# Three pooled means from bands in four buffers with alternating halves, and the decays of linear attention two chunks at a time

## The chip, the cores and the metric

The kernel runs on one core of a Trainium2 chip. The metric is the device time of one launch in microseconds (us), and lower is better. The engines that matter here are TensorE (PE, with its weight loads shown apart as PEld), VectorE (DVE), ScalarE (ACT), GpSimd (POOL) and the DMA queue of SyncE (SP), from which nearly all transfers of this kernel are issued.

## The reference

The reference runs two transformer blocks on 512 latent tokens of width 1024, and in the first block on 256 context tokens too. The change touches the first block alone, which has two layers (0 and 1). The mixer of a layer concatenates three parts and multiplies them by `w_out`: a pooled mean, gated linear attention, and softmax attention of the latent tokens over latent and context keys.

```python
mix = jnp.concatenate([pool_mixer(p, w_pool, s_pool),
                       gla_output(o_gl, gg, g_gla, x.dtype),
                       latent_attention(ql, k_all, v_all)], axis=-1) @ w_out
x = x + ga1 * mix
```

`pool_mixer` takes 256 features in four groups of 64. Each group has a window of its own (2, 4, 8 or 16 tokens); its mean over the window minus the token itself is multiplied by a 64x64 matrix and scaled:

```python
for gi, w in enumerate(POOL_WINDOWS):
    lo = np.clip(t - w // 2, 0, N - 1)
    hi = np.clip(t + w // 2 - 1, 0, N - 1)
    cnt = jnp.asarray((hi - lo + 1)[None, :, None], jnp.float32)
    mean = (Pg[:, hi + 1] - Pg[:, lo]) / cnt
    outs.append(mean - pf[:, :, gi])
```

Gated linear attention has decays `la = log_sigmoid(r @ w_gate + b_gate) / 16`, which are summed up along a chunk; the state is multiplied by the exponential of a chunk's sum from one chunk to the next, forward and backward:

```python
b = jnp.cumsum(lc, axis=2)
S_new = jnp.exp(bl[:, :, 0, :, None]) * S + jnp.einsum('bhjd,bhje->bhde', kc * jnp.exp(bl - b), vc)
```

## The kernel before

Activations are kept transposed, with features on the partitions, and each large product is done as three matmuls of split operands (`dense`, L296 to L298 and their token-major forms; below they are called dense work). The program is written as one list of steps. A scheduler then fixes the order of the instructions on each engine; the engines run their own lists in that order, and wait for each other and for transfers by semaphores. SP's list is such a list too: a DMA whose buffer isn't free yet holds up every DMA behind it.

**The pooled mean** (`pool`, L998 to L1031) is a product with band matrices that hold window, count and the minus one. For each group of 64 features it loads one band tile `bt` of 128x400 (L1008: three variants of a 128x128 band; L1009 and L1010: two edges of eight columns), and for each block of 128 tokens it does one matmul of 128 columns (L1017) and up to two of eight columns for what reaches over the block's edge (L1021, L1024). Two groups share a PSUM bank: one takes partitions 0 to 63, the other 64 to 127. The tag `bt` has one buffer. The two banks come from the tag `mm`, which has two in all and is the one that dense work uses too. Afterwards the two banks are copied (L249, L251), multiplied by the 64x64 matrices in block form (L1030) and scaled (L1031).

`pool` is called three times: for the context in layer 0 (256 tokens, two blocks), for the latents in layer 0 (512 tokens, four blocks), and for the latents in layer 1, in program order behind that layer's attention.

**Around it in layer 0** the kernel still computes the modulation vectors in pieces (L448 loads a quarter of a piece into `mraw`, which has two buffers; L451 multiplies; L460 folds; L462 adds). They all pass through the single bank `at`, as the keys (L865) and the transposed weights (L942) of the context's attention do. The first norm of the latents (L368, L404) takes its sums in the `mm` banks, too. Behind it the dense projections of the latents start.

**Attention** (`attend`) goes through blocks of four heads: scores (L926, L927), row maximum (L928), exponential (L936), transposes through `at` and `op` (L942) into a tile `PT` of six buffers (`weights`, L933), and products with the values (L952), four `PT` tiles a block. In layer 1 it has eight blocks of four heads.

**The decays** (`gla_states`, `sums`) are made chunk by chunk of 128 tokens: Abs (L634), Exp (L635), Ln (L636), four scans (L640), the chunk's sum (L642) and its exponential `dec` (L643). ACT needs an `ACT_TABLE_LOAD` where functions of different tables follow each other.

Of the kernel before, what the change touches and what calls it, by code (L numbers as in the profile page):

```python
# [14 lines left out]
AF = mybir.ActivationFunctionType  # L15
# [177 lines left out]
class Kern:  # L193
# [423 lines left out]
    def gla_states(self, l, o, n, init):  # L617

        nc = self.nc
        nch = n // 128  # L620
        h4 = lambda a: a.rearrange("p (h t) -> p h t", h=4)
        dec = []
        space = self.t([128, 8, 256], "gst")
        bg = self.vec(f"bg{l}")
        o["tot"] = []
        def sums(c):

            zp = self.sm()
            for hh in range(4):
                nc.tensor.matmul(zp[:, hh * 128:(hh + 1) * 128], self.wg[:, hh * 128:(hh + 1) * 128],  # L630
                                 o["r"][:, c * 128:(c + 1) * 128], start=True, stop=True)
            y, a, B = self.w("K"), self.w("Q"), o["B"][c]
            nc.vector.tensor_tensor(h4(y), h4(zp), bg.unsqueeze(2).to_broadcast([128, 4, 128]), op=ALU.add)
            nc.scalar.activation(a, y, AF.Abs)  # L634
            nc.scalar.activation(a, a, AF.Exp, scale=-1.0)  # L635
            nc.scalar.activation(a, a, AF.Ln, bias=1.0)  # L636
            nc.vector.scalar_tensor_tensor(y, y, 0.0, a, op0=ALU.min, op1=ALU.subtract)
            for hh in range(4):
                nc.vector.tensor_tensor_scan(h4(B)[:, hh], self.ones, h4(y)[:, hh], 0.0, op0=ALU.mult, op1=ALU.add)
            tot = self.t([128, 4], "tot", 10)  # L640
            nc.vector.tensor_scalar(tot, h4(B)[:, :, 127], 1.0 / 16, None, op0=ALU.mult)
            d = self.t([128, 4], "dec", 10)  # L642
            nc.scalar.activation(d, tot, AF.Exp)  # L643
            nc.vector.tensor_tensor(B[64:], B[64:], y[64:], op=ALU.subtract)
            dec.append(d)
            o["tot"].append(tot)

        def update(c):

            B, tot = o["B"][c], o["tot"][c]  # L650
            EK = self.w("E")
            for hh in range(4):
                nc.scalar.activation(h4(EK)[:64, hh], h4(B)[:64, hh], AF.Exp, scale=-1.0 / 16, bias=tot[:64, hh:hh + 1])
            nc.scalar.activation(EK[64:], B[64:], AF.Exp, scale=1.0 / 16)
            nc.vector.tensor_tensor(EK, EK, o["kd"][c], op=ALU.mult)
            tp = self.sm()
            for hh in range(4):
                s = slice(hh * 128, (hh + 1) * 128)
                nc.tensor.transpose(tp[:, s], EK[:, s], self.ident)
            KT = self.w("QE")  # L660
            self.copy(KT, tp)
            up = self.sm()
            for hh in range(4):
                nc.tensor.matmul(up[:, hh * 64:(hh + 1) * 64], KT[:, hh * 128:(hh + 1) * 128],
                                 o["gv"][c][:, hh * 64:(hh + 1) * 64], start=True, stop=True)
            self.copy(space[:, 4 + c], up[:, :256])
        sums(0)
        for c in range(nch):
            if c + 1 < nch:
                sums(c + 1)  # L670
            update(c)
        d4 = lambda a: a.rearrange("p (h e) -> p h e", h=4)
        S = [space[:, c] for c in range(nch)]
        fin = self.t([128, 256], "Sfin", 2)
        for half, order in ((slice(0, 64), range(nch)), (slice(64, 128), range(nch - 1, -1, -1))):
            order = list(order)
            if init is None:
                nc.gpsimd.memset(S[order[0]][half], 0.0)
            else:
                nc.vector.tensor_copy(S[order[0]][half], init[half])  # L680
            for i, c in enumerate(order):
                dst = S[order[i + 1]] if i + 1 < nch else fin
                nc.vector.tensor_tensor(d4(dst[half]), d4(S[c][half]),
                                        dec[c][half].unsqueeze(2).to_broadcast([64, 4, 64]), op=ALU.mult)
                nc.vector.tensor_tensor(dst[half], dst[half], space[half, 4 + c], op=ALU.add)
        o["S"] = S
        return fin
# [310 lines left out]
    def pool(self, l, o, n, out):  # L998

        nc = self.nc  # L1000
        ntb = n // 128
        sums = [self.ps()[:, :n] for _ in range(2)]
        for pr in range(2):
            ps = sums[pr]
            for half in range(2):
                gi = pr * 2 + half
                bt = self.t([128, 400], "bt")
                nc.sync.dma_start(bt[:, :384], self.A["bands"][:, gi * 384:(gi + 1) * 384])  # L1008
                nc.sync.dma_start(bt[:, 384:392], self.A["bands"][:, 1536 + gi * 8:1536 + gi * 8 + 8])  # L1009
                nc.sync.dma_start(bt[:, 392:400], self.A["bands"][:, 1568 + gi * 8:1568 + gi * 8 + 8])  # L1010
                r = slice(half * 64, half * 64 + 64)
                ch = slice(gi * 64, gi * 64 + 64)
                for tb in range(ntb):
                    v = 0 if tb == 0 else 2 if tb == ntb - 1 else 1
                    t0 = tb * 128
                    more = (tb > 0) + (tb < ntb - 1)
                    nc.tensor.matmul(ps[r, t0:t0 + 128], o["p"][tb][:, ch], bt[:, v * 128:(v + 1) * 128],  # L1017
                                     start=True, stop=False, skip_group_check=True)
                    if tb > 0:
                        more -= 1  # L1020
                        nc.tensor.matmul(ps[r, t0:t0 + 8], o["p"][tb - 1][:, ch], bt[:, 384:392],  # L1021
                                         start=False, stop=(more == 0), skip_group_check=True)
                    if tb < ntb - 1:
                        nc.tensor.matmul(ps[r, t0 + 120:t0 + 128], o["p"][tb + 1][:, ch], bt[:, 392:400],  # L1024
                                         start=False, stop=True, skip_group_check=True)
        for pr in range(2):
            self.copy(out[pr], sums[pr])
        for pr in range(2):
            yp = self.ps()[:, :n]
            nc.tensor.matmul(yp, self.wp[:, pr], out[pr], start=True, stop=True)  # L1030
            nc.scalar.activation(out[pr], yp, AF.Copy, scale=self.vec(f"s_pool{l}")[:, pr:pr + 1])  # L1031
# [46 lines left out]
    def block1(self):  # L1078
        nc, A = self.nc, self.A
# [21 lines left out]
        def finish(l, j, n, x, hm, hid, tags):  # L1101
# [11 lines left out]
            elif j == 0:  # L1113
# [10 lines left out]
        o = dict(gv=self.take(U, 0, 2, 256), kd=self.take(U, 512, 2, 512), qd=self.take(U, 1536, 2, 512),  # L1124
                 B=self.take(U, 2560, 2, 512), p=self.take(U, 3584, 2, 256), aq0=self.take(U, 4608, 2, 256),
                 aq1=self.take(U, 5120, 2, 256), gg=self.take(U, 5632, 2, 256),
                 kv=self.take(U, 4096, 2, 256), kvs=[U[:, 4096:4608]],
                 aqs=[U[:, 4608:5120], U[:, 5120:5632]])
        self.gla_proj(0, h, NC, o)
        self.masks(o["gv"][1])  # L1130
        self.after(o["gv"][1], self.t([128, 400], "bt")[:, :1])
        self.att_proj(0, h, NC, o)
        self.rest_proj(0, h, NC, o)
        self.ropes(o["gg"][1])
# [35 lines left out]
        for l in range(2):  # L1170
            if l == 0:
                h, U, o = hl, Ul, ol
                self.gla_proj(0, h, NL, o)
            else:
                h, U = self.hpairs(), self.ground()
                first_norm(1, 0, NL, x, h, self.NORM, SPLITS["down0"])
                V, o = arrays(U)
# [14 lines left out]
            if l == 0:  # L1192
# [17 lines left out]
                o = dict(gv=self.take(U, 0, 2, 256), kv=self.take(U, 512, 2, 256), kd=self.take(U, 2048, 2, 512),  # L1210
                         B=self.take(U, 5120, 2, 512), kvs=[U[:, 512:1024]])
# [691 lines left out]
```

## Time and profile before

| what | value |
|---|---|
| median of 3 runs | 3540.68 us (3539.99 to 3544.39) |
| the profiled execution | 3541.75 us, of which 3539.7 us from the first to the last instruction |
| mean granted TensorE clock | 0.961 of full speed |
| busy share of PE, PEld, DVE, ACT, POOL | 94%, 79%, 60%, 46%, 2% |
| instructions | 53711 |

The busy share of PE is an average over the kernel. It is lower in a few stretches of the first block, and the three calls of `pool` lie at 121 to 140 us (context), 247 to 272 us (latents, layer 0) and 1366 to 1388 us (latents, layer 1). A matmul's duration in the rows is longer than the distance to the next one, since matmuls are pipelined; the work that PE does in a stretch is read from the distances of the starts.

### The profile page before, as it was taken

The page shows a single profiled execution, that of the slowest core. Times are in us where ns is not written, and L with a number is a line of the kernel's source. Part 1 is how long each engine was busy: PE and PEld are TensorE (multiplying, and loading weights), DVE is VectorE, ACT ScalarE, POOL GpSimd, SP SyncE. Part 2 cuts the span into 40 slices and gives each one's busy share as a digit, 9 for nine tenths or more (in the row PEclk, how much of TensorE's full clock was granted, in tenths as well). Part 3 has the DMA queues.
Part 4 walks back from the last instruction along what each step waited for, and adds up shares of the span by engine and source line. Part 5 has one row for each costly group of instructions (what it writes and reads, how often), then busy time and mean ns, then how long its engine had stood idle before and what let it go on. Part 6 is the DMA issues. An engine that isn't in the chain of part 4 may idle for free. (4 is left out here: it accounts for less than half of the span.)

```text
span 3539.7 us, 53711 instructions
## 1 busy us (share of the span) xinstructions
PE 3330.4 (94%) x20698; PEld 2811.5 (79%) x20698; DVE 2130.1 (60%) x3914; ACT 1635.7 (46%) x3023; POOL 59.4 (2%) x105
## 2 busy tenths in 40 slices
PE   7898799998999999889999899999999999999998
PEld 5776788887788788777788687778889877888886
DVE  3833898557533448856533668999766436563334
ACT  3513766354333346633333557666554325364332
POOL 0000000000000000000000000000000000000000
PEclk9799899999999999999999899999999999999998
DMA  6443122744632321036632357565666556553222
GB/s 226 136 159 100 60 85 72 238 151 132 194 115 96 109 66 44 9 108 194 201 106 89 112 159 225 169 183 158 206 194 190 176 169 202 159 180 119 95 95 72
DMA packets 267247, 491.44 MB, mean 139 GB/s; under 512 B 44784, under 2 KB 128752, under 8 KB 266736
## 3 DMA queue, kind: packets, MB, share of 16 engines
q1 hardware_dynamic: 212976, 446.06, 39.7%
q10 hardware_dynamic: 54016, 41.95, 3.6%
q8 instruction: 163, 2.67, 0.3%
q14 instruction: 92, 0.75, 0.1%
HBM read 430.11 MB, written 57.80 MB: 138 GB/s over the span
## 5 line engine op out<-in xcount | busy, mean ns | idle before, releaser
L286 DVE TENSOR_TENSOR wlo<-wraw,whi 128x1024 fp32r<-128x1024 f32 x503 | 615.2, 1223 | 574.7 <-ACT whi L285 563.2
L285 ACT ACTIVATE whi<-wraw 128x1024 fp32r<-128x1024 f32 x503 | 531.4, 1056 | 911.9 <-PE mm L297 776.9
L296 PE MATMUL mm<-h,whi 128*128 128x512 f32 (+1 forms) x2344 | 862.0, 370 | 30.8 <-ACT h L419 8.4
L297 PE MATMUL mm<-h,whi 128*128 128x512 f32 (+1 forms) x2344 | 854.0, 365 | 16.9 <-DVE h L420 13.1
L298 PE MATMUL mm<-h,wlo 128*128 128x512 f32 (+1 forms) x2344 | 838.4, 365 | 7.8 <-DVE wlo L286 7.7
L296 PEld LDWEIGHTS mm<-h,whi 128*128 128x128 f32 x2344 | 447.6, 192 | 113.6 <-ACT h L419 11.5
L297 PEld LDWEIGHTS mm<-h,whi 128*128 128x128 f32 x2344 | 449.0, 192 | 94.8 <-DVE h L420 20.9
L298 PEld LDWEIGHTS mm<-h,wlo 128*128 128x128 f32 x2344 | 446.2, 191 | 81.3 <-DVE wlo L286 10.7
L296 PE MATMUL mm<-whi,h 128*128 128x256 f32 x1200 | 350.7, 295 | 11.2 <-ACT whi L285 8.3
L297 PE MATMUL mm<-wlo,h 128*128 128x256 f32 x1200 | 349.7, 292 | 11.8 <-DVE wlo L286 11.4
L298 PE MATMUL mm<-whi,h 128*128 128x256 f32 x1200 | 345.3, 289 | 0.0
L296 PEld LDWEIGHTS mm<-whi,h 128*128 128x128 f32 x1200 | 231.0, 194 | 28.1 <-ACT whi L285 10.6
L297 PEld LDWEIGHTS mm<-wlo,h 128*128 128x128 f32 x1200 | 232.6, 194 | 21.9 <-DVE wlo L286 17.9
L298 PEld LDWEIGHTS mm<-whi,h 128*128 128x128 f32 x1200 | 232.2, 193 | 14.1 <-issue 11.2
L296 PE MATMUL mm<-U,whi 128*128 128x512 f32 (+1 forms) x608 | 229.1, 377 | 3.2 <-DVE V L1075 3.2
L297 PE MATMUL mm<-U,whi 128*128 128x512 f32 (+1 forms) x608 | 227.2, 374 | 0.0
L298 PE MATMUL mm<-U,wlo 128*128 128x512 f32 (+1 forms) x608 | 223.8, 377 | 0.0
L488 DVE SCALAR_TENSOR_TENSOR AT<-mraw,cst,AT 128x512 f32<-128x512 f32 x140 | 105.0, 750 | 100.7 <-DMA mraw<-in_w_ada 62.0
L1285 DVE SCALAR_TENSOR_TENSOR fa<-fr,const,fa 128x511 f32<-128x511 f32 (+2 forms) x192 | 142.9, 753 | 22.8 <-ACT fa L1280 20.3
L296 PE MATMUL mm<-big,whi 128*128 128x512 f32 x384 | 153.2, 399 | 2.7 <-DVE fa L1817 1.8
L297 PE MATMUL mm<-big,whi 128*128 128x512 f32 x384 | 152.8, 398 | 0.0
L298 PE MATMUL mm<-big,wlo 128*128 128x512 f32 x384 | 149.2, 397 | 0.0
(531 smaller groups left out, 5017.3 us busy)
## 6 DMA issues: line engine op xcount, KB each, us to landing
wraw<-in_w_in SPq DMA_DIRECT2D x166, 512.0 KB, 3.9
wraw<-in_w_up SPq DMA_DIRECT2D x96, 512.0 KB, 3.4
wraw<-in_w_down SPq DMA_DIRECT2D x96, 512.0 KB, 3.4
mraw<-in_w_mod SPq DMA_DIRECT2D x96, 256.0 KB, 3.1
mraw<-in_w_ada SPq DMA_DIRECT2D x96, 256.0 KB, 3.0
wraw<-in_w_out SPq DMA_DIRECT2D x40, 512.0 KB, 3.3
wraw<-in_w_mlp_up SPq DMA_DIRECT2D x40, 512.0 KB, 3.3
mraw<-in_w_late SPq DMA_DIRECT2D x64, 256.0 KB, 2.9
```

Of the source, the lines that this page charges most:

```text
L285: nc.scalar.activation(hi, raw, AF.Copy)
L286: nc.vector.tensor_tensor(lo, raw, hi.bitcast(F32), op=ALU.subtract)
L296: nc.tensor.matmul(out, lh, rh, start=start, stop=False)
L297: nc.tensor.matmul(out, lh, rl, start=False, stop=False)
L298: nc.tensor.matmul(out, ll, rh, start=False, stop=stop)
L488: nc.vector.scalar_tensor_tensor(acc, raw, st[:, k, 0:1], acc, op0=ALU.mult, op1=ALU.add)
L1285: nc.vector.scalar_tensor_tensor(acc[:, d:], raw[:, :NL - d], w(j), acc[:, d:], op0=ALU.mult, op1=ALU.add)
```

## The change

The band tiles of all four groups get buffers of their own. They are four tiles of the tag `PT`, which has six buffers and belongs to attention. Each is first written in one column by a copy on POOL from `gg[1]` (`after`, L526), so that it isn't loaded before that projection is there, and then loaded by three DMAs; all twelve DMAs are issued ahead of the matmuls. The matmuls then go over token blocks and steps, and the two groups that share a bank alternate from one instruction to the next. The number of matmuls, their sizes and their sums are what they were. A gate of the old single buffer (`after(o["gv"][1], ...)`, L1131) is gone.

In the decays, `sums` ends behind Exp, `logs` does what follows, and `pair` calls `sums` for two chunks and then `logs` for both. The exponential of the chunk's sum moves into `update`.

```diff
-        sums(0)
-        for c in range(nch):
-            if c + 1 < nch:
-                sums(c + 1)
+
+        def pair(c):
+            for i, ya in enumerate([sums(c), sums(c + 1)]):
+                logs(c + i, *ya)
+        pair(0)
+        for c in range(0, nch, 2):
+            if c + 2 < nch:
+                pair(c + 2)
             update(c)
+            update(c + 1)
...
         sums = [self.ps()[:, :n] for _ in range(2)]
+        bands = []
+        for gi in range(4):
+            bt = self.t([128, 768], "PT", 6)[:, :400]
+            self.after(o["gg"][1], bt[:, :1])
+            nc.sync.dma_start(bt[:, :384], self.A["bands"][:, gi * 384:(gi + 1) * 384])
+            nc.sync.dma_start(bt[:, 384:392], self.A["bands"][:, 1536 + gi * 8:1536 + gi * 8 + 8])
+            nc.sync.dma_start(bt[:, 392:400], self.A["bands"][:, 1568 + gi * 8:1568 + gi * 8 + 8])
+            bands.append(bt)
         for pr in range(2):
-            ps = sums[pr]
-            for half in range(2):
-                gi = pr * 2 + half
-                bt = self.t([128, 400], "bt")
...
+            for tb in range(ntb):
...
+                for i, (b, to, c) in enumerate(steps):
+                    for gi, r in both:
+                        nc.tensor.matmul(ps[r, to], o["p"][b][:, gi * 64:gi * 64 + 64], bands[gi][:, c],
+                                         start=(i == 0), stop=(i == len(steps) - 1), skip_group_check=True)
...
         self.masks(o["gv"][1])
-        self.after(o["gv"][1], self.t([128, 400], "bt")[:, :1])
```

Three places of the order show what the scheduler makes of it. The first is SP's list at the latents' pool of layer 0. A name's number is one tile: `bt_2064`, `bt_2078` are two users of the one buffer, `PT_2052` to `PT_2067` are four tiles in four buffers, `mraw` is a piece of modulation weights. In the square brackets is what the instruction waits for. Before:

```order
L1008 DMA bt_2064<-in_bands 128x384 [waits DMAHW7_49,PE_49]
L1009 DMA bt_2064<-in_bands 128x8
L1010 DMA bt_2064<-in_bands 128x8
L284 DMA wraw_3007<-in_w_in 128x1024 [waits DVE_49]
L448 DMA mraw_1172<-in_w_mod 128x512 [waits DMAHW5_49,PE_49]
L448 DMA mraw_1176<-in_w_mod 128x512 [waits DMAHW6_49,DMAHW4_49,PE_49]
L1008 DMA bt_2078<-in_bands 128x384 [waits DMAHW1_49,DMAHW7_49,DMAHW0_49,PE_49]
L1009 DMA bt_2078<-in_bands 128x8
L1010 DMA bt_2078<-in_bands 128x8
L448 DMA mraw_1180<-in_w_mod 128x512 [waits DMAHW3_49,PE_49]
```

Now:

```order
L1017 DMA PT_2057<-in_bands 128x8
L1016 DMA PT_2052<-in_bands 128x384 [waits Pool_49]
L1016 DMA PT_2057<-in_bands 128x384 [waits DMAHW3_49,Pool_49]
L1018 DMA PT_2057<-in_bands 128x8 [waits DMAHW4_49]
L1016 DMA PT_2062<-in_bands 128x384 [waits Pool_49]
L1017 DMA PT_2062<-in_bands 128x8
L1018 DMA PT_2062<-in_bands 128x8 [waits DMAHW7_49]
L1016 DMA PT_2067<-in_bands 128x384 [waits DMAHW0_49,Pool_49]
L448 DMA mraw_1112<-in_w_mod 128x512 [waits DMAHW1_49,PE_49]
L448 DMA mraw_1116<-in_w_mod 128x512 [waits DMAHW2_49,PE_49]
L1017 DMA PT_2067<-in_bands 128x8 [waits DMAHW3_49]
L1018 DMA PT_2067<-in_bands 128x8 [waits DMAHW4_49]
```

Before, each load of a band waited for PE's matmuls with the band before it, and the loads of modulation pieces stood behind it in the list. Now all four bands stand together, wait for the copies on POOL, and are in the list some 15 rows earlier.

The second place is PE's list in the same pool. `mm_2048` and `mm_2050` are the first of its two banks, `mm_2049` and `mm_2051` the second; 64x128 is a matmul of 128 columns. Before, one band's matmuls followed each other, with modulation pieces (L451, L460) between the bands, here between the second and the third:

```order
L1017 MATMUL mm_2048<-bt_2064,U_297_1469 64x128
L1021 MATMUL mm_2048<-bt_2064,U_297_1469 64x8
L460 MATMUL at_1149<-const_69,mrow_1166 128x2 x2
L451 MATMUL at_1171<-mraw_1172,cst_72 32x256 x2
L451 MATMUL at_1171<-mraw_1176,cst_72 32x256 x2
L1017 MATMUL mm_2049<-bt_2078,U_297_1469 64x128
L1024 MATMUL mm_2049<-bt_2078,U_297_1469 64x8
```

Now the two bands of a bank take turns, and the third and fourth band follow the first two at once:

```order
L1033 MATMUL mm_2050<-PT_2052,U_296_1471 64x8
L1033 MATMUL mm_2050<-PT_2057,U_296_1471 64x8
L1033 MATMUL mm_2051<-PT_2062,U_296_1471 64x128
L1033 MATMUL mm_2051<-PT_2067,U_296_1471 64x128
L1033 MATMUL mm_2051<-PT_2062,U_296_1471 64x8
L1033 MATMUL mm_2051<-PT_2067,U_296_1471 64x8
```

From the pool's first matmul to its last, ten rows of L451 and two of L460 stood between its own rows before; two of L451 and one of L460 are left there, and the others stand behind the pool now.

The third place is PE's list where layer 1's attention ends (`op_13107` and `op_13113` are the last block's products with the values, `at_...` the reciprocals of its sums, `h_...` the mixed features that go into `w_out`). Before, the pool's matmuls, both L1030 and 36 dense matmuls of 512 columns stood inside the attention, and dense work followed its end at once:

```order
L952 MATMUL op_13107<-PT_13176,V_1889_11240 64x128
L952 MATMUL op_13107<-PT_13188,V_1889_11240 64x128
L960 MATMUL at_13225<-const_69,inv_13226 128x128 x2
L296 MATMUL mm_14208<-h_2352_14169,whi_14241 128x512
L296 MATMUL mm_14209<-h_2352_14169,whi_14241 128x512
L297 MATMUL mm_14208<-h_2352_14169,whi_14241 128x512
```

Now nothing of the pool and no dense matmul of `w_out` stands inside the attention; all of the pool stands behind it, and then the dense work:

```order
L961 MATMUL op_13113<-PT_13182,V_1888_11246 64x128
L961 MATMUL op_13113<-PT_13194,V_1888_11246 64x128
L969 MATMUL at_13231<-const_69,inv_13232 128x128 x2
L1033 MATMUL mm_14075<-PT_14077,U_1865_11164 64x128
L1033 MATMUL mm_14075<-PT_14082,U_1865_11164 64x128
L1033 MATMUL mm_14075<-PT_14077,U_1865_11164 64x8
```

SP's list there, with the `PT` buffers that the last two attention blocks had (the first two tiles follow the last but one block, the other two the last):

```order
L1017 DMA PT_14077<-in_bands 128x8 [waits DVE_49,PE_49,Activation_49]
L1016 DMA PT_14077<-in_bands 128x384 [waits Pool_49]
L1018 DMA PT_14077<-in_bands 128x8 [waits DMAHW7_49]
L1016 DMA PT_14082<-in_bands 128x384 [waits DMAHW0_49,Pool_49]
L1017 DMA PT_14082<-in_bands 128x8 [waits DMAHW1_49]
L1018 DMA PT_14082<-in_bands 128x8 [waits DMAHW2_49]
L1017 DMA PT_14087<-in_bands 128x8 [waits DVE_49,DMAHW3_49,PE_49,Activation_49]
L1016 DMA PT_14087<-in_bands 128x384 [waits DMAHW4_49,Pool_49]
```

What moved here is the whole third pool, with all that has to wait for its two banks: its loads now wait for the attention's last products.

In the decays the order on ACT keeps the `ACT_TABLE_LOAD`s: 25 in the whole kernel before and 25 now. The Ln of a pair's first chunk still stands between the Exps of the two chunks, with a load on each side.

## Rows read from the trace of the kernel before

**Rows 1.** Busy time by stretch: PE, PEld, DVE, ACT, POOL; then granted clock, DMA share, GB/s.

```profile
120.00:168.00 48.00, 42.80 (x317) 33.36 (x315) 40.61 (x97) 19.23 (x50) 6.44 (x11) 0.70 0.42 135
...
247.00:280.00 33.00, 27.84 (x178) 16.79 (x179) 4.61 (x11) 3.30 (x5) 0.00 (x0) 0.64 0.49 152
...
1360.00:1530.00 170.00, 148.66 (x1386) 125.44 (x1385) 143.72 (x281) 104.99 (x242) 10.43 (x20) 0.96 0.07 20
```

**Rows 2.** Timeline of the context pool in layer 0.

```profile
121.47 0.43 PE L1017 MATMUL mm<-bt,U 128*64 128x128 f32 x2
...
129.45 0.69 PE L1017 MATMUL mm<-bt,U 128*64 128x128 f32 x2 [0.91 <-DMA bt<-in_bands]
...
139.11 0.38 ACT L249 ACTIVATE U<-mm 128x256 f32<-128x256 f32 x1 [6.01 <-PE mm L1021]
```

**Rows 3.** Timeline of PE behind it: the first dense work of the latents.

```profile
168.18 0.58 PE L296 MATMUL mm<-whi,h 128*128 128x256 f32 x1
```

**Rows 4.** SP queue's waits, 100 to 300 us: line, what for, us, times, longest.

```profile
SPq L448 <- PE at L451: 67.0, 40, 5.0
```

**Rows 5.** Timeline of the latents' pool in layer 0, all engines.

```profile
246.56 0.28 PE L297 MATMUL mm<-wlo,h 128*128 128x256 f32 x1
...
246.68 0.28 PE L298 MATMUL mm<-whi,h 128*128 128x256 f32 x1
...
246.89 0.43 PE L1017 MATMUL mm<-bt,U 128*64 128x128 f32 x2
...
247.24 0.41 PE L1017 MATMUL mm<-bt,U 128*64 128x128 f32 x2
...
247.49 0.23 PE L1021 MATMUL mm<-bt,U 128*64 128x8 f32 x2
...
247.65 0.64 PE L451 MATMUL at<-mraw,cst 128*32 128x256 f32 x8
...
252.09 1.73 PE L451 MATMUL at<-mraw,cst 128*32 128x256 f32 x8 [2.80 <-DMA mraw<-in_w_mod]
...
253.74 0.69 PE L1017 MATMUL mm<-bt,U 128*64 128x128 f32 x2
...
256.93 0.33 SPq L1008 DMA_DIRECT2D bt<-in_bands  x1
...
271.48 3.78 PE L1030 MATMUL mm<-U,lw 128*128 128x512 f32 x4
```

**Rows 6.** Landing time of the band loads (L1008).

```profile
DMA to landing us min/median/max: 2.3/2.4/3.9
```

**Rows 7.** Context attention: the scores of the 16 heads, first and last start.

```profile
L926 PE MATMUL S<-K,q x16: 279/365/582, 310.7 to 351.7; 128*128 128x256 f32 x16
```

**Rows 8.** Timeline of PE there: two heads' scores.

```profile
342.51 0.38 PE L926 MATMUL S<-K,q 128*128 128x256 f32 x1 [0.48 <-ACT P L936]
...
344.38 0.36 PE L926 MATMUL S<-K,q 128*128 128x256 f32 x1
```

**Rows 9.** Timeline of PE there: the work that follows.

```profile
360.12 1.65 PE L630 MATMUL sm<-oo,lw 128*128 128x128 f32 x6 [1.96 <-ACT oo L249]
```

**Rows 10.** Timeline of PE at the end of layer 1's attention.

```profile
1518.91 0.62 PE L296 MATMUL mm<-h,whi 128*128 128x512 f32 x2
...
1527.23 1.04 PE L952 MATMUL op<-PT,V 128*64 128x128 f32 x16
1528.10 0.61 PE L952 MATMUL op<-PT,vc 128*64 128x128 f32 x8
...
1531.68 0.73 PE L296 MATMUL mm<-h,whi 128*128 128x512 f32 x2 [1.46 <-ACT h L259]
...
1533.22 0.39 PE L297 MATMUL mm<-h,whi 128*128 128x512 f32 x1
1533.45 0.39 PE L298 MATMUL mm<-h,wlo 128*128 128x512 f32 x1
```

**Rows 11.** Table loads of Ln, by its line.

```profile
L636 ACT ACT_TABLE_LOAD  x12: 1283/1283/1283, 81.1 to 1350.3; - x12
```

More of the change, by code (lines that the diff above doesn't have):

```diff
@@ L631, in sums @@
                                  o["r"][:, c * 128:(c + 1) * 128], start=True, stop=True)
-            y, a, B = self.w("K"), self.w("Q"), o["B"][c]
+            y, a = self.w("K"), self.w("Q")
             nc.vector.tensor_tensor(h4(y), h4(zp), bg.unsqueeze(2).to_broadcast([128, 4, 128]), op=ALU.add)
@@ L635, in sums, with logs @@
             nc.scalar.activation(a, a, AF.Exp, scale=-1.0)
+            return y, a
+        def logs(c, y, a):
+            B = o["B"][c]
             nc.scalar.activation(a, a, AF.Ln, bias=1.0)
@@ L641, in sums @@
             nc.vector.tensor_scalar(tot, h4(B)[:, :, 127], 1.0 / 16, None, op0=ALU.mult)
-            d = self.t([128, 4], "dec", 10)
-            nc.scalar.activation(d, tot, AF.Exp)
             nc.vector.tensor_tensor(B[64:], B[64:], y[64:], op=ALU.subtract)
-            dec.append(d)
             o["tot"].append(tot)
@@ L650, in update @@
             B, tot = o["B"][c], o["tot"][c]
+            d = self.t([128, 4], "dec", 10)
+            nc.scalar.activation(d, tot, AF.Exp)
+            dec.append(d)
             EK = self.w("E")
@@ L1002, in pool @@
         sums = [self.ps()[:, :n] for _ in range(2)]
-        for pr in range(2):
-            ps = sums[pr]
-            for half in range(2):
-                gi = pr * 2 + half
-                bt = self.t([128, 400], "bt")
[L1008 to L1025, printed above, removed]
@@ new lines, in pool @@
+        bands = []
[6 more added lines that the diff above has]
+            bands.append(bt)
+        for pr in range(2):
+            ps, both = sums[pr], [(pr * 2 + half, slice(half * 64, half * 64 + 64)) for half in range(2)]
+            for tb in range(ntb):
+                v = 0 if tb == 0 else 2 if tb == ntb - 1 else 1
+                t0 = tb * 128
+                steps = [(tb, slice(t0, t0 + 128), slice(v * 128, (v + 1) * 128))]
+                if tb > 0:
+                    steps.append((tb - 1, slice(t0, t0 + 8), slice(384, 392)))
+                if tb < ntb - 1:
+                    steps.append((tb + 1, slice(t0 + 120, t0 + 128), slice(392, 400)))
+                for i, (b, to, c) in enumerate(steps):
+                    for gi, r in both:
+                        nc.tensor.matmul(ps[r, to], o["p"][b][:, gi * 64:gi * 64 + 64], bands[gi][:, c],
+                                         start=(i == 0), stop=(i == len(steps) - 1), skip_group_check=True)
```

## The prediction

> **What bounds the kernel now.** I read the table of busy time by stretch first, then the timeline of each stretch with a pool in it. Over the kernel PE is the bound, so only those stretches count in which PE loses time, and the table shows two of them around the first two pools [rows 1]. From 120 to 168 us PE is busy for 42.80 us, but at 0.70 of the full clock: some 30 us of work at full speed, so that 18 of 48 us are lost. From 247 to 280 us it is busy for 27.84 us at 0.64, some 18 us of work in 33 us, so that 15 us are lost. The stretch of layer 1's attention is another matter: PE 148.66, DVE 143.72 of 170 us, clock 0.96.
>
> The timelines show what the reader is to see there. The context's pool starts at 121.47 us, waits for a band at 129.45 and gives its banks free at 139.11, when the copies read them [rows 2]: 17.6 us for eight groups of matmuls. The first dense work of the latents comes at 168.18 us [rows 3], since their first norm needs the two `mm` banks that the pool holds. The latents' pool of layer 0 lasts from 246.89 to 271.48 us, where L1030 follows: 24.6 us [rows 5]. At full clock a 128-column product (two instructions) takes 0.25 us from start to start (247.24 to 247.49), and one with its eight-column product 0.35 (246.89 to 247.24), so that an edge takes 0.10. The later ones run at half clock: the row that lasted 0.43 us lasts 0.69. In between PE waits 2.80 us for a piece of modulation weights (252.09): the SP queue had not issued it yet, for it stood behind a band's loads that waited for PE. At 256.93 us the next band is issued at last, right behind the last matmul with the one before. SP's own table says the same: loads of modulation pieces waited 67.0 us for PE at L451 [rows 4]. So the pool and the modulation take turns through one queue and one buffer each, and the clock falls meanwhile.
>
> **The change, part by part.**
>
> *A, the context's pool.* The twelve loads stand early in SP's list and wait for POOL's copies only. The pool's matmuls can follow each other from 123 us or so. Eight products with eight edges are 8 x 0.35 = 2.8 us at full clock [rows 5] and 6 at half, so the banks come free near 128 instead of 139.1, 11 us earlier. The chain from there to the dense work (29 us, [rows 2, 3]) has its own waits on DVE, which is busy for 40.61 of the 48 us [rows 1], so it won't shrink much by itself. What stood in it and is now later in PE's order (some 6 us of linear attention and modulation) is hidden in dense work at first, but costs PE its time. Bounds: 0, if DVE holds the chain in place, and -18, all that is lost. I take -10, near the 11 us by which the banks are early.
>
> *B, the latents' pool, layer 0.* It has 16 products and 24 edges: 16 x 0.25 + 24 x 0.10 = 6.4 us at full clock. Eight of the ten L451 rows of the order (two rows are the x8 that took 0.64 us, [rows 5]) and an L460 of about 0.5 move behind the pool, 3.1 us of work. What is left inside, two L451 rows and an L460, is 1.1 us more, so the 24.6 us become about 6.4 + 1.1, less the alternation, and 3.1 us are paid later: -14 to -16. L1030 ran 3.78 us for four at the falling clock [rows 5]; without the fall this gives another 1 or 2. I take -16; bounds -6 (the pool still waits for its bands or for the moved pieces) and -19 (all 15 lost us and the alternation).
>
> *Alternation.* What two halves of the array do in turn is seen in L952, which has the same shape and alternates already: 16 matmuls from 1527.23 to 1528.10, 54 ns each [rows 10], against 125 ns for those of the pool at full clock (0.25 us for two, [rows 5]). For the 32 instructions of a latents' pool that is worth 32 x 0.071 = 2.3 us, and 1.1 us for the 16 of the context's. The Trainium skill, "TensorE: Matmul & The Clock Gate", Part 3: Packing small matmuls, says that a weight load overlaps matmuls in flight only when the row group differs, and these differ in the column group; by that the alternation would be worth nothing and the sum 5.7 us higher. The rows of L952 speak against it. The 2.3 and 1.1 us are within the -16 and -10 above.
>
> *What is given back in layer 0.* The pieces of modulation are later in PE's order against the dense work, and the context's attention waits for the last of them, since both use the bank `at`. So less dense work lies beside that attention: by the order 39 dense matmuls of 256 columns between L865 and the first L630 instead of 156. The 117 at 0.12 us (246.56 to 246.68, [rows 5]) are 14 us that come ahead of it now. Its 16 heads start at 310.7 and 351.7 us [rows 7], 2.7 us apart on the mean; alone they run at 1.87 us (342.51 to 344.38, [rows 8]), 31 us in all, and L630 follows at 360.12 [rows 9]. So it gets shorter by (2.73 - 1.87) x 15 = 13 us at best, which would pay for nearly all of those 14, or by nothing. I take +4, bounds 0 and +14. From there on PE is full, and what is won by L630 stays: -10 - 16 + 4 = -22.
>
> *C, the pool of layer 1.* Here `PT` decides. Two of the four tiles take buffers that the last but one attention block had, two those of the last, so the loads wait for the last products with the values. Before, dense work came back at 1531.68 us, 2 us behind the last L952, and all of the pool and 36 dense matmuls had been done inside the attention [rows 10]. Now follow, behind the end of the values: a copy on POOL (an estimate of 0.5), six more issues on SP at 0.33 or a little more (2.3, [rows 5]), landing (2.4, [rows 6]), the second bank's matmuls (2.1 at full clock), the copy of 512 columns (0.7, by 0.38 for 256 in [rows 2]), L1030 (0.95, [rows 5]) and its scaling (0.7): 10 us until dense work can start, which is 8 more than before, and 1 or 2 more at half clock. The 36 dense matmuls at 0.23 us (1533.22 to 1533.45, [rows 10]) are 8.3 us that now come after. That is +17 or +18. On the other side PE has 8.3 + 6.4 + 2 = 17 us less to do within the 170 us of the attention. DVE is busy for 143.72 of them, and the heads' own chain lies over that; so the attention gets shorter by something between 0 and 17. I take 7, since PE's 149 and DVE's 144 us are close. C = +10, bounds 0 and +18. If the tiles had been free earlier, this cover would have stayed, and C would be about -2.
>
> *Decays.* The Ln loads of the table are 12 at 1.283 us [rows 11], and by the order no load is saved; `dec` moves behind, its 0.2 us is off the path. 0, within 3 either way where ACT works between attention's exponentials. The dropped copy and the new ones on POOL lie in an idle engine: 0, except in C, where one is counted.
>
> Sum: -22 + 10 + 0 = -12 on 3541.75 us of the profiled execution: 3529.75. That execution is 1.07 us above the median, so 3528.7 for the median. **I say 3529 us.**
>
> **The rivals.** *The attention of layer 1 gives all back* (PE-bound there): C is 0, and the time 3519. For it: PE 149 of 170 us is the largest; against: a head's chain through four engines. *The early gain is swallowed.* DVE (40.61 of 48) holds the context stretch, A is near 0 or -3, and the shortened attention doesn't pay: the net by L630 is -9 or -10, C takes it, and the time is 3540.7, no change. For it: the first dense work already lay 29 us behind the pool. *Slower.* One mechanism: the loads of modulation pieces, two buffers and SP's order, set when the context's attention may start (67.0 us of waits, [rows 4]), and it starts at 310.7 as now and takes as long. Then nothing of A and B is left by L630, C costs +10, and the time is 3551. It decides so if the first L926 stays within 3 us of 310.7. Against it: by the rows PE, not SP's landing, was late in most of those waits (SP waited for PE's L451). *The alternation does nothing*, and 125 ns an instruction stay: 5.7 us more, 3534.4. That is what the named rule of the Trainium skill would make of it. *The decays don't do what they say*: that is in the sum, as 0.
>
> **How the numbers follow.** Chances: my forecast with its alternation 0.48, PE-bound attention 0.14, swallowed 0.20, slower 0.10, no alternation 0.08. Range 3513 to 3546: below, the second with the best of A and B; above, half way to the slower one. A measurement of this kernel can tell about 0.2%, 7 us. Faster than 3533.6: the forecast for the most part, the PE-bound case and some of the last, 0.64; within: 0.25; slower than 3547.8: 0.11.
>
> **What would show it.** A: the first dense work of the latents near 157 instead of 168.18, with the clock above 0.70. B: pool and its waits within 8 us, no wait at L451 within it. Alternation: near 55 ns between the starts of 128-column matmuls. Layer 0: L630 some 22 us earlier than 360.12. C: a gap on PE of 6 to 10 us between the attention's last products and L1030, and dense work 12 us after them. The prediction is wrong if L630 comes less than 12 us earlier, or if the gap in layer 1 isn't there.

## The result, and the profile of the changed kernel

The changed kernel takes 3562.12 us at the median of 4 runs (3554.66 to 3567.65), the kernel before 3540.34 (3537.19 to 3544.39): a ratio of 1.0052 with a 95% interval of [1.0028, 1.0075]. It is slower, and the forecast of 3529 us (3513 to 3546) was wrong. The profiled execution took 3567.65 us, with a span of 3565.9.

The same stretches in the table of busy time by stretch, after the change, with one more for the context's attention (312 to 363 us; columns as in [rows 1]):

```profile
120.00:168.00 48.00, 42.66 (x350) 34.25 (x350) 43.63 (x100) 19.84 (x51) 5.64 (x10) 0.84 0.38 127
247.00:280.00 33.00, 31.85 (x270) 22.59 (x266) 5.71 (x12) 4.75 (x7) 0.00 (x0) 1.00 0.50 166
312.00:363.00 51.00, 37.08 (x201) 29.80 (x202) 26.47 (x82) 21.29 (x62) 0.00 (x0) 0.64 0.10 41
1360.00:1530.00 170.00, 137.21 (x1251) 115.13 (x1249) 137.04 (x270) 98.69 (x228) 11.17 (x24) 0.91 0.05 14
```

The first two lines answer to [rows 1]. The stretches of the first two pools lose less than before: the clock is 0.84 instead of 0.70 in the one and 1.00 instead of 0.64 in the other, where PE now is busy for 31.85 of 33 us. The third line shows what it cost: beside the context's attention PE is busy for 37.08 of 51 us at a clock of 0.64. In layer 1 PE has 11 us less work in the same 170 us, at 0.91 instead of 0.96.

The timeline of PE at the latents' pool of layer 0, and below it the first dense work of the latents:

```profile
243.37 0.84 PE L1033 MATMUL mm<-PT,U 128*64 128x128 f32 x16
244.15 0.63 PE L451 MATMUL at<-mraw,cst 128*32 128x256 f32 x4
244.70 0.62 PE L1033 MATMUL mm<-PT,U 128*64 128x8 f32 x12
245.25 0.63 PE L451 MATMUL at<-mraw,cst 128*32 128x256 f32 x4
245.81 2.12 PE L1033 MATMUL mm<-PT,U 128*64 128x8 f32 x46
247.86 0.61 PE L460 MATMUL at<-const,mrow 128*128 128x2 f32 x4
248.40 0.50 PE L1033 MATMUL mm<-PT,U 128*64 128x128 f32 x6
248.83 1.13 PE L1039 MATMUL mm<-U,lw 128*128 128x512 f32 x2
```

```profile
147.50 0.39 PE L296 MATMUL mm<-whi,h 128*128 128x256 f32 x1
```

The pool lasts from 243.37 to 248.83 us where it lasted from 246.89 to 271.48 [rows 5], with three rows of modulation work within it (L451 twice, L460 once), and nothing waits. The first dense work comes at 147.50 instead of 168.18 us [rows 3], 20.7 us earlier; the second pool starts only 3.5 us earlier. When L594 starts behind the pool (252.09 against 275.73), the changed kernel is 23.6 us ahead.

Three more stretches, columns as above: from the first dense work to the second pool, before and after the change, and after the change from L594 to the transposes of the context's keys (L874).

```profile
168.18:246.89 78.71, 78.02 (x653) 67.12 (x649) 33.81 (x80) 18.52 (x32) 0.00 (x0) 0.99 0.46 149
...
147.50:243.37 95.87, 89.59 (x749) 73.87 (x748) 47.86 (x108) 25.17 (x51) 3.17 (x9) 0.96 0.45 146
...
252.09:304.30 52.21, 49.72 (x407) 38.66 (x407) 9.88 (x19) 9.81 (x15) 0.00 (x0) 1.00 0.46 149
```

Then the context's attention: its scores (L935 is L926 of before), and PE's timeline of the last fold of a modulation piece, of two heads, and of L630.

```profile
L935 PE MATMUL S<-K,q x16: 364/562/583, 313.3 to 350.3; 128*128 128x256 f32 x16
```

```profile
301.33 0.61 PE L460 MATMUL at<-const,mrow 128*128 128x2 f32 x4
...
320.86 0.37 PE L935 MATMUL S<-K,q 128*128 128x256 f32 x1
...
322.58 0.44 PE L951 MATMUL op<-const,P 128*128 128x128 f32 x2 [1.24 <-ACT P L945]
322.78 0.37 PE L935 MATMUL S<-K,q 128*128 128x256 f32 x1
...
359.42 1.16 PE L630 MATMUL sm<-oo,lw 128*128 128x128 f32 x8 [2.05 <-ACT oo L249]
```

The last fold stands at 301.33 us, the first scores at 313.3 (before: 310.7, [rows 7]), and L630 at 359.42 (before: 360.12, [rows 9]). All but 0.7 of the 23.6 us are gone. A head waits for its exponential (L945), with no dense work to put into the wait.

The end of layer 1's attention, on PE and on the SP queue:

```profile
1529.18 1.04 PE L961 MATMUL op<-PT,V 128*64 128x128 f32 x16
1530.15 0.71 PE L969 MATMUL at<-const,inv 128*128 128x128 f32 x4
1530.79 2.09 PE L1033 MATMUL mm<-PT,U 128*64 128x128 f32 x42
1534.33 2.81 PE L1033 MATMUL mm<-PT,U 128*64 128x128 f32 x38 [1.46 <-DMA PT<-in_bands]
1537.08 2.51 PE L1039 MATMUL mm<-U,lw 128*128 128x512 f32 x4
1540.16 1.08 PE L296 MATMUL mm<-h,whi 128*128 128x512 f32 x2 [0.58 <-ACT h L259]
```

```profile
1516.61 0.33 SPq L1017 DMA_DIRECT2D PT<-in_bands  x1
...
1528.98 0.33 SPq L1017 DMA_DIRECT2D PT<-in_bands  x1
...
1531.51 0.43 SPq L1018 DMA_DIRECT2D PT<-in_bands  x1
```

Before, the last products with the values were here:

```profile
1528.54 1.04 PE L952 MATMUL op<-PT,V 128*64 128x128 f32 x16
```

They start at 1529.18 now, 0.6 us later, although layer 1 had begun 2 us earlier. The second pair of bands is loaded from 1528.98 on, PE waits for it until 1534.33, and dense work comes back at 1540.16 instead of 1531.68 [rows 10].

Places of the work in single profiles, in us from the start (a kernel's times in one execution; between executions they move by some us):

| kernel | first dense of the latents | second pool's L1030 | context's scores, first | latents' L630 | layer 1: dense resumes | median of runs, ratio |
|---|---|---|---|---|---|---|
| before | 168.2 | 271.5 | 310.7 | 360.1 | 1531.7 | 3540.34 |
| changed | 147.5 | 248.8 | 313.3 | 359.4 | 1540.2 | 3562.12, 1.0052 |
| c_only | 165.9 | 269.1 | 308.3 | 358.0 | 1538.2 | 3563.59, 1.0050 |
| l1_own | 149.9 | 252.6 | 316.9 | 362.6 | 1542.2 | 3547.15, 1.0011 |
| late4 | 146.9 | 248.0 | 268.7 | 328.2 | 1554.0 | 3574.75, 1.0090 |
| drop4_before | 168.7 | 271.2 | 269.7 | 339.7 | 1514.9 | 3529.23, 0.9955 |
| drop4_l1_own | 150.9 | 252.6 | 273.8 | 330.1 | 1489.4 | 3507.75, 0.9895 |
| moved4_before | 167.2 | 268.8 | 267.3 | 338.6 | 1514.0 | 3537.61, 0.9993 |
| moved4_l1_own | 145.7 | 247.9 | 268.7 | 325.1 | 1509.9 | 3524.80, 0.9956 |

Ratios are to runs of the kernel before on the same chip, whose median lay between 3540.3 and 3544.9. Where dense work resumes in layer 1, the changed kernel, c_only and late4 still have 36 dense matmuls to do that the kernel before and l1_own have behind them.

My theory after the profile: the 17 to 18 us of layer 1 are the price of the `PT` buffers alone, and the early gain is lost because the context's attention starts when the modulation pieces are through, which it did at the same time as before. The main rival: there is only so much dense work to lie beside layer 0's chains, and what is used early is missing later, whatever the pieces do.

### The profile page after: what moved, and what is told of

It reads as the page before. It is cut to its first block, busy times and chain, and to the rows that moved or that the text cites. A ratio compares the mean times of both kernels' runs of the same rounds, so it can differ in the third digit from the quotient of the medians.

```text
span 3565.9 us, 53736 instructions
## 1 busy us (share of the span) xinstructions
PE 3334.0 (93%) x20698; PEld 2816.2 (79%) x20698; DVE 2130.7 (60%) x3914; ACT 1639.8 (46%) x3023; POOL 64.1 (2%) x116
```

## Experiments

**Layer 1's bands in own buffers (l1_own).**

```diff
-            bt = self.t([128, 768], "PT", 6)[:, :400]
+            bt = self.t([128, 400], "bt", 2) if l else self.t([128, 768], "PT", 6)[:, :400]
```

> The changed kernel, but the third pool (layer 1) has its bands in two buffers of its own instead of attention's PT buffers; order of the second block as in the kernel before. Theory: the PT buffers alone pushed that pool and 36 dense matmuls behind the attention (+17 to +18 us), so this kernel has the pool inside the attention again, dense work resumes 2 us behind its last products, and the time is 3540, within 4 of the kernel before (the early gain stays lost at the context's attention). Rival 1 (the decays, not the buffers, lengthen layer 1's attention): the time stays at 3555 to 3562. Rival 2 (the early gain is kept and layer 1 alone cost more than it): 3515 to 3525.

Measured: 3547.15 us, ratio 1.0011 [0.9998, 1.0023]: no difference to the kernel before that can be told. The pool is inside the attention again, and dense work follows the last values as before:

```profile
1539.03 1.04 PE L961 MATMUL op<-PT,V 128*64 128x128 f32 x16
...
1542.17 0.73 PE L296 MATMUL mm<-h,whi 128*128 128x512 f32 x2 [1.46 <-ACT h L259]
```

**The third pool alone (c_only).** The kernel before, in which only the call of `pool` in layer 1 is the new one.

```diff
-                self.pool(1, o, NL, mp)
+                self.pool_ahead(1, o, NL, mp)
```

> The kernel before, in which the third pool alone is done as in the change (four PT buffers, alternating halves); the two pools of layer 0 and the decays are as before. Theory: +17 us at the end of layer 1's attention, 3557, and up to 9 more if the other order of the second block costs what the trace of the changed kernel shows there. Rival (the cost needs the other edits): within 5 us of the kernel before.

Measured: 3563.59 us, ratio 1.0050 [1.0030, 1.0070], as much as the change as a whole cost. The end of the attention looks like that of the changed kernel:

```profile
1529.72 0.71 PE L960 MATMUL at<-const,inv 128*128 128x128 f32 x4
1530.37 2.01 PE L1060 MATMUL mm<-PT,U 128*64 128x128 f32 x42
...
1538.15 1.08 PE L296 MATMUL mm<-h,whi 128*128 128x512 f32 x2 [0.58 <-ACT h L259]
```

**The decays alone (decays).** The kernel before with the change's `gla_states`.

> The kernel before with the decays of the change alone (two chunks at a time); pools as before. Theory: no table load is saved, nothing on the path moves: 3540 within 4 us, up to 5 either way in the second block, whose order comes out different. Rival (the decays cost what the changed kernel lost beyond the pools): 3546 to 3552. If they did what they say, and saved table loads on the path: 3532 or less.

Measured: 3544.40 us, ratio 0.9999 [0.9985, 1.0013]: no difference that can be told.

**Without alternation (noalt).**

```diff
-            for tb in range(ntb):
+            for half, tb in [(hf, tb) for hf in range(2) for tb in range(ntb)]:
...
-                    for gi, r in both:
+                    for gi, r in both[half:half + 1]:
```

> The changed kernel with the bands still loaded ahead, but each band's matmuls one after the other (no alternating of the halves). Theory (two column halves of the array work at the same time): the latents' pool of layer 0 takes 6.4 us of PE's time instead of the 3.5 to 4.1 that the trace of the changed kernel shows, and the starts of 128-column instructions are 0.125 us apart again. Rival (weight loads overlap only across row groups, the alternation is worth nothing): the same 3.5 to 4.1 us. The whole time can't tell 6 us apart in one run.

Measured: 3550.01 us in one run, and PE's timeline of the same pool:

```profile
239.64 0.84 PE L1033 MATMUL mm<-PT,U 128*64 128x128 f32 x8
240.41 0.63 PE L451 MATMUL at<-mraw,cst 128*32 128x256 f32 x4
240.96 0.62 PE L1033 MATMUL mm<-PT,U 128*64 128x8 f32 x6
241.51 0.62 PE L451 MATMUL at<-mraw,cst 128*32 128x256 f32 x4
242.06 3.62 PE L1033 MATMUL mm<-PT,U 128*64 128x8 f32 x56
245.62 0.61 PE L460 MATMUL at<-const,mrow 128*128 128x2 f32 x4
246.16 0.95 PE L1033 MATMUL mm<-PT,U 128*64 128x128 f32 x10
247.04 1.01 PE L451 MATMUL at<-mraw,cst 128*32 128x256 f32 x8
```

From start to start the four groups of its matmuls take 0.77 + 0.55 + 3.56 + 0.88 = 5.76 us; in the changed kernel 0.78 + 0.55 + 2.05 + 0.43 = 3.81. So the alternation is worth 2.0 us in a latents' pool. That the two column halves work at the same time is the reason given for it; no run shows it apart from the shorter distances. The whole time of this kernel lies under the four runs of the changed one, but it is a single run, and nothing follows from it.

**Four modulation pieces held back (late4).** Changed kernel.

```diff
-        self.tick(16)
+        self.tick(12)
+        held, self.later = self.later, []
...
         self.attend(0, o, NC, [(kc, vc, NC)], None, ma)
+        self.later += held
```

> The changed kernel, with the last 4 of layer 0's 16 modulation pieces issued behind the context's attention instead of ahead of it. Theory: the pieces keep a pace of 11.4 us each whatever the pools do and the context's attention waits for the last of them, so that it started at 313 us and ran alone at half clock. With 4 fewer ahead its first scores come some 45 us earlier, near 268, dense work lies beside it, and of the 23 us that layer 0 was ahead at 250 us at least 12 are still there when the latents' attention of layer 0 starts: total 3545 to 3550, 12 to 17 under the changed kernel. Rival (the attention's own chain and the clock take the time back wherever it lies): 3558 to 3564, as the changed kernel.

Measured: 3574.75 us, ratio 1.0090 [1.0069, 1.0111]. The place was right: first scores at 268.7 us, and L630 31 us earlier. The time was not. `tick` issues one piece for each step of the next projection, which has three, so the fourth came behind the latents' attention (its loads and matmuls at 577.82 and 581.70 us), and the context's MLP, which needs it, did too. Beside the latents' attention of layer 0 there was almost no dense work left (13 dense matmuls from 460 to 580 us, 440 in the changed kernel):

```profile
460.00:500.00 40.00, 33.85 (x327) 27.68 (x326) 36.78 (x68) 23.16 (x56) 2.62 (x5) 1.00 0.10 34
500.00:540.00 40.00, 33.59 (x327) 28.92 (x326) 35.27 (x75) 25.24 (x61) 3.23 (x7) 0.96 0.05 15
540.00:580.00 40.00, 28.99 (x258) 22.69 (x258) 18.54 (x63) 19.83 (x43) 0.00 (x0) 0.91 0.17 47
```

In the kernel before PE is busy for 36.73, 39.84 and 40.00 us in those three stretches. A held piece is as good a gate there as in front of the context's attention.

**Four pieces left out, with the old and with the new pools (drop4_before, drop4_l1_own).** Both without the pieces of one vector; the second with own buffers in layer 1.

```diff
-        for i in range(2, 6):
+        for i in range(2, 5):
             part(0, i, "at")
-        self.tick(16)
+        M[0][5] = M[0][2]
+        self.tick(12)
```

> The kernel before without the last 4 of layer 0's 16 modulation pieces (the gate of the second residual takes the values of the first one's; 4 x 2.6 us of PE work and 16 loads less). Theory: the context's attention starts when the pieces are through, about 44 us earlier in their own pace, but here the latents' pool ends only at 272, so its first scores come near 283 instead of 310.7; with dense work beside it all along. Time 3522 to 3532.

> The changed kernel with layer 1's bands in own buffers, and without the same 4 modulation pieces. Theory: with the pieces out of the way the early gain is not lost at the context's attention; its first scores come near 268, L630 of the latents some 10 us before that of the other kernel without the 4 pieces, and the time is 5 to 12 us under it. Rival (there is only so much dense work to lie beside the chains of layer 0, and what is used early is missing later, whatever the pieces do): both kernels without pieces within 4 us.

Measured: 3529.23 us, ratio 0.9955 [0.9939, 0.9970], and 3507.75 us, ratio 0.9895 [0.9879, 0.9912]: 21 us between them. First scores and L630 with the old pools:

```profile
L926 PE MATMUL S<-K,q x16: 285/365/1058, 269.7 to 323.5; 128*128 128x256 f32 x16
...
L630 PE MATMUL sm<-oo,lw x16: 272/346/421, 339.7 to 344.0; 128*128 128x128 f32 x16
```

and with the new ones:

```profile
L935 PE MATMUL S<-K,q x16: 281/364/415, 273.8 to 322.7; 128*128 128x256 f32 x16
...
L630 PE MATMUL sm<-oo,lw x32: 272/275/579, 330.1 to 355.1; 128*128 128x128 f32 x32
```

Without the pieces in front, the scores of the old kernel start 41 us earlier, when its second pool ends (I had said 283 and got 269.7). L630 comes 9.6 us earlier with the new pools, and the first norm of layer 1 (L368) 15.0 us (1180.3 against 1195.3); with all pieces in front it starts at 1219.2 before, 1217.5 in the changed kernel and 1221.1 in l1_own. The whole time is 21 us lower at the median, more than the 5 to 12 expected, and 12 us between the two profiled executions. The rival, that both come out within 4 us, falls. Each edit also lets the scheduler order the rest anew, so a comparison of two kernels holds that too.

**Three buffers for the modulation weights, kernel before (mraw3_before).** `mraw` has 3 buffers instead of 2.

> The kernel before with three buffers for pieces of modulation weights instead of two, pools and decays as before. Theory (the pace of 11.4 us a piece comes from two buffers and their loads): 7 to 10 us a piece, the last piece well before 301 us, first scores of the context's attention 8 or more us before 310.7, and the time some 3 to 8 us lower. Rival (the pace is PE's, whose list is full): no change of the pace, 3540 to 3544.

Measured: 3551.37 us, ratio 1.0012 [0.9997, 1.0028].

```profile
L926 PE MATMUL S<-K,q x16: 277/372/582, 304.9 to 351.6; 128*128 128x256 f32 x16
```

The last fold comes at 291.3 us instead of 301.1, the 15 distances from 127.1 on are 10.9 us on the mean instead of 11.5, and the first scores come 5.9 us earlier. The last scores (351.6) and L630 (359.9) stay where they were. So the two buffers have a small part in the pace of the pieces, but are not what sets it, and an earlier start of the attention alone brings nothing here.

**Four pieces moved, all at once (moved4_l1_own, moved4_before).** As late4, with `self.tick(4)` behind `self.later += held`, on the changed kernel with own buffers in layer 1 and on the kernel before.

> The changed kernel with layer 1's bands in own buffers, and with the last 4 of layer 0's modulation pieces issued all at once behind the context's attention (in the kernel that held back 4, one of them came only behind the latents' attention, and no dense work of the context's MLP could lie beside that). Theory: first scores of the context's attention near 270, dense work inside the latents' attention of layer 0 again, and most of the 21 us that leaving the pieces out gave between the two kernels without them are kept: 3518 to 3530 against 3544 for the kernel before. Rival (the pieces in the one bank hold up the latents' attention instead): 3540 or more.

> The kernel before with the same 4 modulation pieces issued behind the context's attention; pools and decays as before. Theory: part of the gain comes from moving the pieces alone, and the pools' part stays out: 3530 to 3540, at least 6 us over the kernel that has both. Rival (moving the pieces is all of it): the same time as the kernel with the new pools in layer 0, within 4 us.

Measured: 3524.80 us, ratio 0.9956 [0.9940, 0.9973], and 3537.61 us, ratio 0.9993 [0.9980, 1.0006]. With the new pools:

```profile
L935 PE MATMUL S<-K,q x16: 281/366/415, 268.7 to 317.7; 128*128 128x256 f32 x16
...
L630 PE MATMUL sm<-oo,lw x32: 273/275/487, 325.1 to 343.7; 128*128 128x128 f32 x32
```

With the old ones:

```profile
L926 PE MATMUL S<-K,q x16: 285/365/683, 267.3 to 319.9; 128*128 128x256 f32 x16
...
L630 PE MATMUL sm<-oo,lw x24: 270/275/356, 338.6 to 369.7; 128*128 128x128 f32 x24
```

Moving the pieces does nothing for the kernel before that can be told in the whole time. In its profile L630 comes 21.5 us earlier than without the move, and layer 1's first norm 15.1 us (1204.1 against 1219.2), but only 7 us of this are left at the end of the two profiles and 3 between the medians; why is not shown. With the new pools in layer 0 the time is 13 us lower than that, and layer 1's first norm comes 14.3 us earlier (1189.8 against 1204.1).

**Versions that go on from there (moved4_old_decays, moved4_mraw3).** New pools in layer 0 alone, old third pool, old decays, moved pieces; and the same with three `mraw` buffers.

> The kernel before with the new pools in layer 0 alone, the third pool and the decays as before, and the 4 modulation pieces moved behind the context's attention. Theory: decays and alternating halves in layer 1 add nothing, so this is the same as the kernel with the moved pieces and the change's decays: 3520 to 3530. Rival (the decays two chunks at a time gave part of that gain): 3532 or more.

> The same, with three buffers for the modulation weights instead of two. By the run of the kernel before with three buffers (no gain): within 4 us of the kernel with two. If the pace of the pieces still holds the context's attention: 5 us less.

Measured: 3523.51 us, ratio 0.9943 [0.9923, 0.9963], and 3511.44 us, ratio 0.9920 [0.9902, 0.9938]. The first is as expected: the decays had no part in it. The second is 12 us under it at the median, against both the expectation and the run with three buffers alone; the intervals overlap a little. The traces show where it helps: the stretch from the first dense work to the second pool takes 87.5 us with three buffers (147.84 to 235.34) instead of 96.3 with two (148.09 to 244.43). In the kernel before, whose PE is busy for 78.02 us of that stretch, it takes 78.8 us with three and 78.7 with two. No further run was made for this. The kernel moved4_mraw3 is the fastest version that leaves nothing out, 0.8% under the kernel before.

## Why the prediction was wrong

*A and B held in their sum, and that by luck.* Together they were to be 26 us, and 23.6 were there at L594. A was to be 10. The banks came free early as said: L1030 of the context's pool came 14.4 us earlier (125.98 against 140.36), where 11 were forecast, and the first dense work 20.7 us earlier, past the bound of 18. But of that only 3.5 us were left when the second pool started, and in l1_own, with the same two pools, none (247.14 against 246.89). The work that had stood in the context's stretch now stands among the dense work: 749 matmuls in 95.87 us instead of 653 in 78.71, 479 of them dense in both, and 5.9 us of waits instead of 0.7. I had put this work at some 6 us; the stretch got 17 us longer. So A came out where the rival "swallowed" had it, though DVE didn't hold the dense work back as that rival has it. B was to be 16 with a bound of 19, and brought 20.1 from the pool's start to L594 (28.84 us before, 8.72 after), because the pieces moved out of it are paid for only behind L594. The clock rose as said.

*The alternation held*, with 2.0 us for the 2.3 forecast. The rule that was weighed against it, from the Trainium skill, "TensorE: Matmul & The Clock Gate", Part 3: Packing small matmuls, is on weight loads, and I had read it to mean that column groups gain nothing by turns; the runs disagree with that reading, 3.81 against 5.76 us.

*The step that failed is "What is given back in layer 0".* I gave it +4 with bounds of 0 and +14; it was +23. Two things were wrong in it. First, only the 117 dense matmuls that come ahead of the attention were priced, at 14 us; what came ahead was 25 us of work. PE's rows between L594 and the first transposes of the context's keys (L865, now L874) show the rest: before, 144 dense matmuls and 32 of L451 in 27 us; now 261 and 72, and 20 transposes of a projection (L581), in 52 us. The pieces that A and B had pushed out of the pools came back here, 6 us of them, and 2 us of folds with them. So the start of the attention stayed where the pieces end. They are 11.4 us apart on the mean from 130.7 to 301.3, and were 11.5 apart from 128.0 to 301.1. Second, the attention alone is hardly faster than with dense work beside it: 37.0 us from the first to the last scores instead of 41.0, with PE idle for its exponentials and a clock of 0.64. I had taken some 10 us for that, from heads 1.87 us apart [rows 8] (16 of them are 30 us, not 31); but these are two of one block, and the last eight heads of the kernel before, which already ran with no dense work beside them, are 2.14 us apart on the mean (336.78 to 351.73), those of the changed kernel 2.47. In sum: 25.1 us more up to the keys, 1.1 more up to the first scores, 3.3 less from there to L630. So the cover was lost and little came back for it: 12 dense matmuls lie between the first scores and L630, where 108 lay before.

This is the rival "slower", with its condition: the first scores were to stay within 3 us of 310.7, and they came at 313.3. Its reason was half right. The pieces do set the start: without 4 of them, or with 4 moved, it is 41 to 48 us earlier with the old pools and the new, and then 204 dense matmuls lie between the first scores and L630 with the new pools, 302 with the old. But the two buffers have only a small part in it, as mraw3_before shows. In the stretch that ends at the keys PE is busy for 49.72 of 52.21 us at a clock of 1.00, and only 1.7 us of its waits are for pieces (at L451). There it is PE's own full list, in which the last piece stands that late, that holds the attention back. What made the scheduler put the pieces at this distance (the one bank, or the dense work between them) remains open.

*C had its mechanism right; its size came out near the upper bound.* I took +10 between bounds of 0 and +18. In the two profiles it is 16.8 us: dense work resumes 8.5 us later (forecast: 8 to 10), and 36 dense matmuls, 8.3 us, are behind it. In the runs of c_only it is 18 us by the ratio, and 11 to 25 by its interval. l1_own and c_only show that the buffers' tag does it: ratio 1.0011 for the changed kernel without the tag, and 1.0050 with the third pool alone. The term in doubt is the attention, which should get shorter by 7 us for having 17 us less to do on PE. Between the two profiles its last products come no earlier. Other profiles don't bear that out: from the first scores to the last products with the values, the attention took 168.6 to 182.4 us in the eight kernels that have the pool and all 36 dense matmuls inside it (before has the 168.6, l1_own 176.7), and 166.8 to 170.6 in the four that have them behind (changed 170.6). So it may well get shorter, by up to some 9 us on the mean, and the profile of the kernel before is the shortest of its kind. How much it gives back remains open. Some 9 of the 26 us between the two profiled executions lie in the second block, 1573.4 us before and 1582.7 after; late4 has the changed kernel's order on PE there and took 1575.8, so that is the spread between executions.

*Decays:* 0, as said; the profile after counts 12 table loads for Ln as before.

The sum as it came out: -23.6 at L594, +23 at the context's attention, +17 to +18 in layer 1, 0 for the decays. The sign that I had named for being wrong, L630 less than 12 us earlier, is there with 0.7 us.

## What to carry to other kernels

Time won in one stretch is kept only if the next gate opens earlier too. Ask what the next stretch that hides work under itself is waiting for (here the last of a row of small pieces in PE's list), and whether the work that hid it will still be there; four pieces moved behind it turned no gain at all (l1_own) into one of 0.4%. A buffer that is borrowed from another stage's tag brings that stage's last reader along: with two buffers of its own the third pool cost nothing that could be told. And count all that is displaced in the order, the small work too.

## What the runs showed that I had not expected

PE work beside chains costs less than its own time: with 96 dense matmuls less beside it, some 11 us of PE's work, the context's attention got only 3.3 us shorter up to L630, at a clock of 0.64 instead of 0.90. Executions of one kernel differ by more than its first runs told: the kernel before took 3529.76 to 3559.62 us over the jobs, and layer 1's stretch from its norm to the next one took 341 to 356 us in the profiles of the ten kernels that have their third pool inside the attention (341 is the kernel before), and 353 to 359 in the four that have it behind. One profile of each kernel can't tell a difference of some 10 us there; the runs' medians could.
